# Latent attention on one core: product order and true widths of the narrow blocks

## The chip, the cores and the metric

The kernel runs on 1 core of a Trainium2 chip. The metric is the device time of one execution in microseconds (us), the median of several runs. Five engines work side by side and wait for each other by semaphores: PE multiplies matrices, DVE and ACT work on elements, POOL does a little of the same, SP issues the DMA transfers.

## The reference

Two layers of a decoder. Each normalises its input, projects it, sends it through three branches (a state-space mixer, latent attention, a gated DeltaNet), merges them by gates and ends with a feed-forward block. The change lies in the latent attention, which has 8 heads over 512 tokens in blocks of 128:

```python
sc = (jnp.einsum('bqhd,bkhd->bhqk', qn, k_nope, preferred_element_type=jnp.float32)
      + jnp.einsum('bqhr,bkr->bhqk', qp, k_pe, preferred_element_type=jnp.float32))
...
sc = jnp.where(kpos[None, :] <= qpos[:, None], sc * scale, -jnp.inf)
pr = jax.nn.softmax(sc, axis=-1)
return jnp.einsum('bhqk,bkhd->bqhd', pr.astype(v.dtype), v)
```

Two of the 192 score channels' parts matter below: 128 plain channels, and 64 rotated ones (`k_pe`, shared by all heads).

## The kernel before

All weights and activations are float32. A large product is made from three products of type float32r (float32 rounded to fewer mantissa bits): each operand is split into a high part (rounded by ACT) and a low part (the rest, by DVE), and high by high, high by low and low by high are added in PSUM. Lines 198 to 200 are these three products of the dense layers (`mm3`), lines 170 and 171 the two halves of a weight's split, lines 267 and 268 those of an activation's (`split_act`). Transposes and the small products of the other branches are in plain float32.

The latent attention of a layer works on four pairs of heads (`hp` 0 to 3). For a pair, three dense products give the plain queries of both heads and their rotary part (`pp`). The rotary part goes through a chain of its own: ACT scales it (`qp`, line 620), four DMAs swap its halves (line 545, inside `rope`), DVE rotates it (547 to 549), two DMAs move its 64 rows to the other half of the partitions (line 625), and ACT and DVE put the stacked operands `qps` and `qpl` together (629 to 631). Then keys and values are computed, and each head of the pair goes through these steps:

- Scores: for query block t = 0 to 3, five float32r products (lines 662 to 666) add into one PSUM bank over the first (t + 1) x 128 keys. Lines 665 and 666 are the rotary ones and read `qps` and `qpl`. For t = 0 the products cover 256 keys, of which the second 128 are not used afterwards.
- Softmax: DVE adds the causal mask and takes the extremum (671), ACT the exponential with its sum (673), DVE the reciprocal and the scaling (674, 675). The tile of block t is `pn` t.
- Transposes (683): ten blocks of 128 x 128 in three groups by key block: key block 0 (four of them), key block 1 (three), and key blocks 3 and 2 together (three).
- Split of each group into `th` and `tl` (267, 268): the tiles `mix` for key blocks 0 and 1, the tiles `pt` for blocks 3 and 2.
- Values: for each key block three float32r products (699 to 701) add into the bank `yt`, over the query blocks from that key block on: 512, 384 and 256 columns. Key block 3 has 128 true columns. `pt` has 128 zeroed columns ahead of them (line 577), and the products of block 3 cover 256.

In all there are 4 pairs, 2 heads and 2 layers, so 16 passes of these steps. The order of the instructions on each engine isn't the order of the code. A scheduler sets it when the kernel is built, from its own estimates of each instruction and from priorities: products that are ready at that time, above all the dense products of the next pair or the next branch, are put between the products of a head that still has to wait. SP issues its DMAs in one row, and one that waits for its buffer holds up those behind it. Weights are loaded into `wraw`, which has two buffers.

Line 570 is used as a measuring mark in the prediction: it is four plain float32 products of one column each per layer:

```python
for t in range(T):
    behind(((ly, "q", 0), 3, 2), pe.matmul(ps[:, t : t + 1], cq_sq[0][:, t * P : (t + 1) * P], ones[:, 0:1], start=True, stop=True))
```

Of the kernel before, what the change touches and what calls it, by code (L numbers as in the profile page):

```python
# [11 lines left out]
F32R = mybir.dt.float32r  # L12
# [8 lines left out]
P = 128  # L21
S = 512
T = S // P
# [32 lines left out]
def hybrid_kernel(ctx, tc, a, out, depth=2, taps=None):  # L56
    nc = tc.nc
    pe, act, dve, pool, sync = nc.tensor, nc.scalar, nc.vector, nc.gpsimd, nc.sync
    uid = itertools.count()

    def mk(pl, shape, dt, tag, bufs=None):
        return pl.tile(shape, dt, tag=tag, name=f"{tag}_{next(uid)}", bufs=bufs)
# [5 lines left out]
    def f32(ap):  # L68
        return ap.bitcast(F32)
# [195 lines left out]
    def split_act(hi, lo, src):  # L265
        with tc.high_priority(30):
            act.copy(hi, src)
            dve.tensor_tensor(lo, src, f32(hi), ALU.subtract)
# [112 lines left out]
    for ly in range(depth):  # L381
# [172 lines left out]
        ps = sm_bank()  # L554
# [17 lines left out]
        rsq(q_rs, ps[:, :T], 1.0 / 512, EPS)  # L572
        dve.tensor_scalar(q_rs, q_rs, -1.0, None, ALU.mult)

        pts = [mk(ml, [P, S], F32R, f"pt{i}") for i in range(2)]
        for x in pts:
            pool.memset(f32(x[:, :P]), 0.0)

        qpl = [mk(ml, [P, S], F32R, f"qpl{j}") for j in range(2)]
        for j in range(2):  # L580
# [4 lines left out]
        for hp in range(4):  # L585
            def q_weights():
                for k0 in (0, 2):
                    raw = mk(wp, [P, 768], F32, "wraw", 2)
                    sync.dma_start(raw.rearrange("p (k n) -> p k n", k=2),
                                   a["mla_w_uq"][ly][k0 * P : (k0 + 2) * P, hp * 384 : (hp + 1) * 384].rearrange("(k p) n -> p k n", p=P))  # L590
                    for k in range(2):
                        rv = raw[:, k * 384 : (k + 1) * 384].rearrange("p (h n) -> p h n", h=2)
                        hi = mk(wp, [P, 384], F32R, "whi")
                        lo = mk(wp, [P, 384], F32R, "wlo")
                        nv = lambda x: x[:, :256].rearrange("p (h n) -> p h n", h=2)
                        pv = lambda x: x[:, 256:].rearrange("p (h n) -> p h n", h=2)
                        act.copy(nv(hi), rv[:, :, :P])
                        act.copy(pv(hi), rv[:, :, P:])
                        dve.tensor_tensor(nv(lo), rv[:, :, :P], f32(nv(hi)), ALU.subtract)
                        dve.tensor_tensor(pv(lo), rv[:, :, P:], f32(pv(hi)), ALU.subtract)  # L600
                        yield k0 + k, hi.unsqueeze(1), lo.unsqueeze(1)

            *pq, pp = dense_F(q_weights(), tiles(384), 512, cqh, cql, tag=(ly, "q", hp))

            def head_tiles(pss, nm, c=None):
                res = []
                for ps in pss:
                    hi = mk(ml, [P, S], F32R, nm + "h", 3)
                    lo = mk(ml, [P, S], F32R, nm + "l", 3)
                    if c is None:  # L610
                        split_act(hi, lo, ps)
                    else:
                        act.mul(hi, ps, c)
                        dve.scalar_tensor_tensor(lo, ps, c, f32(hi), ALU.mult, ALU.subtract)
                    res.append((hi, lo))
                return res

            qs = head_tiles(pq, "q", scale)
            qp = mk(ml, [P, S], F32, "qp")
            act.mul(qp, pp, scale)  # L620
            qr = rope(qp)

            qd = mk(lp, [P, S], F32, "mix", 8)
            for i in range(2):
                sync.dma_start(qd[64 * i : 64 * i + 64], qr[64 * (1 - i) : 64 * (1 - i) + 64])
            qps = [mk(ml, [P, S], F32R, f"qps{j}") for j in range(2)]
            for j in range(2):
                half, other = (slice(64 * i, 64 * i + 64) for i in (j, 1 - j))
                act.copy(qps[j][half], qr[half])
                dve.tensor_tensor(qpl[j][half], qr[half], f32(qps[j][half]), ALU.subtract)  # L630
                act.copy(qps[j][other], qd[other])
            wkv = list(weights(a["mla_w_ukv"][ly], hp * 512, 512, 256))
            with tc.high_priority(30):
                ks = head_tiles(dense_F(wkv, [slice(0, P), slice(256, 256 + P)], 256, ckh, ckl), "k")

            vs = []
            for j in range(2):
                if hp % 2 == 0:
                    v2 = [mk(ml, [P, S], F32R, nm, 2) for nm in ("vh", "vl")]
                elif hp == 1:  # L640
                    v2 = [mk(lp, [P, S], F32R, f"y{e}{6 + j}") for e in "hl"]
                else:
                    v2 = [mk(ml, [P, S], F32R, f"cq{e}{j}") for e in "hl"]
                vs.append([x.rearrange("p (t n) -> p t n", t=T) for x in v2])

            def ev(t, ps):
                for j in range(2):
                    split_act(*(x[:, t, :] for x in vs[j]), ps[:, j * P : (j + 1) * P])

            vcols = lambda w: w.rearrange("p (h n) -> p h n", h=2)[:, :, P:]  # L650
            dense_T(wkv, 256, 256, ckh, ckl, ev, vcols)

            for j in range(2):
                qh, ql = qs[j]
                kh, kl = ks[j]
                pn = []
                for t in range(T):
                    n = max(256, (t + 1) * P)
                    tok = slice(t * P, (t + 1) * P)
                    ps = sm_bank()  # L660
                    o = ps[:, :n]
                    pe.matmul(o, qh[:, tok], kh[:, :n], start=True, stop=False)
                    pe.matmul(o, qh[:, tok], kl[:, :n], start=False, stop=False)
                    pe.matmul(o, ql[:, tok], kh[:, :n], start=False, stop=False)
                    pe.matmul(o, qps[j][:, tok], kps[:, :n], start=False, stop=False)
                    pe.matmul(o, qpl[j][:, tok], kph[:, :n], start=False, stop=True)
                    n = (t + 1) * P
                    o = ps[:, :n]
                    mx = mk(sp, [P, 1], F32, "mx", 8)
                    pt_ = mk(ml, [P, (t + 1) * P], F32, f"pn{t}", 2)  # L670
                    dve.tensor_tensor_reduce(pt_[:, :n], o, causal[:, S - n :], q_rs[:, t : t + 1], 3.0e38, ALU.add, ALU.min, mx)
                    sm = mk(sp, [P, 1], F32, "sme", 8)
                    act.activation(pt_[:, :n], pt_[:, :n], AF.Exp, bias=mx, scale=-1.0, accum_out=sm)
                    dve.reciprocal(sm, sm)
                    dve.tensor_scalar(pt_[:, :n], pt_[:, :n], sm, None, ALU.mult)
                    pn.append(pt_)
                po = y_bank()
                for kbs in ((0,), (1,), (3, 2)):
                    ps = sm_bank()
                    n = 0  # L680
                    for kb in kbs:
                        for t in range(kb, T):
                            pe.transpose(ps[:, n : n + P], pn[t][:, kb * P : (kb + 1) * P], ident)
                            n += P
                    if len(kbs) == 1:
                        th = mk(lp, [P, n], F32R, "mix", 8)
                        tl = mk(lp, [P, n], F32R, "mix", 8)
                        split_act(th, tl, ps[:, :n])
                        parts = [(kbs[0], kbs[0] * P, 0)]
                    else:  # L690

                        th, tl = pts
                        split_act(th[:, P:], tl[:, P:], ps[:, :n])
                        parts = [(2, 2 * P, 2 * P), (3, 2 * P, 0)]
                    for kb, c0, c in parts:
                        v_h, v_l = (x[:, kb, :] for x in vs[j])
                        o = po[:, c0:]
                        w = S - c0
                        pe.matmul(o, v_h, th[:, c : c + w], start=kb == 0, stop=False)
                        pe.matmul(o, v_h, tl[:, c : c + w], start=False, stop=False)  # L700
                        pe.matmul(o, v_l, th[:, c : c + w], start=False, stop=kb == T - 1)
                yh[2 * hp + j], yl[2 * hp + j] = (mk(lp, [P, S], F32R, f"y{e}{2 * hp + j}") for e in "hl")
                split_act(yh[2 * hp + j], yl[2 * hp + j], po)
                tap(f"oT{2 * hp + j}", f32(yh[2 * hp + j]))
            if hp == 0:
                dec, ndec, beta, dtq, dsk = step_sizes()
# [762 lines left out]
```

## Time and profile before

| | us |
|---|---|
| median of 3 runs (2276.94 to 2280.28) | 2278.16 |
| time of the profiled execution | 2278.48 |
| its span, first to last instruction | 2276.7 |
| latent attention, first layer (about 60 to 200 of the span) | 140 |
| latent attention, second layer (about 1190 to 1325) | 135 |

In the rows of a timeline the first number is the start in us from the span's start, the second the duration; `x5` means five instructions shown as one row. The brackets at a row's end say how long the engine was idle ahead of it and what ended the wait. Products overlap in PE's pipeline, so the pace of a stream of them is read from one start to the next and not from the durations. Line numbers are those of the kernel before.

### The profile page before, as it was taken

What the parts mean: (1) busy time and instruction counts of PE and PEld (TensorE: products, weight loads), DVE (VectorE), ACT (ScalarE), POOL (GpSimd) and SP (SyncE); (2) the same over time, 40 slices, a digit from 0 to 9 for tenths busy, and PEclk for the clock granted to TensorE, in tenths of its full rate; (3) what the DMA queues carried; (4) which work ended last, traced back from release to release, by engine and by line L of the source; (5) the groups of instructions that cost most, each with busy time, mean ns of one, the idle gap of its engine ahead of it and who ended that gap; (6) DMA issues with size and microseconds to landing.
All of it is one profiled execution on the core that took longest, in us unless ns stands there. A gap on an engine that the chain in (4) does not pass through costs nothing. (4 is left out here: it accounts for less than half of the span.)

```text
span 2276.7 us, 32125 instructions
## 1 busy us (share of the span) xinstructions
PE 2254.7 (99%) x11758; PEld 1868.6 (82%) x11758; DVE 1647.8 (72%) x3315; ACT 1182.9 (52%) x2444; POOL 65.0 (3%) x84
## 2 busy tenths in 40 slices
PE   9999999999999999999999999999999999999998
PEld 8888787888888888888888878888888887888886
DVE  7786567876667778767868865678657667778668
ACT  6666744333443465554656667443335445645545
POOL 1000000000000000000010000000001000000000
PEclk9999999999999999999999999999999999999999
DMA  4223634452225143233132236335422251432231
GB/s 143 81 75 102 195 102 121 129 148 75 83 68 176 56 148 111 91 99 117 48 104 81 70 113 202 96 118 148 121 84 75 66 184 38 167 111 101 85 111 47
DMA packets 220030, 244.07 MB, mean 107 GB/s; under 512 B 34256, under 2 KB 172384, under 8 KB 219872
## 3 DMA queue, kind: packets, MB, share of 16 engines
q1 hardware_dynamic: 219872, 242.02, 34.6%
q8 instruction: 92, 1.51, 0.3%
q14 instruction: 66, 0.54, 0.1%
HBM read 225.53 MB, written 11.74 MB: 104 GB/s over the span
## 5 line engine op out<-in xcount | busy, mean ns | idle before, releaser
L170 ACT CAST whi<-wraw 128x512 fp32r<-128x512 f32 (+1 forms) x536 | 329.3, 618 | 536.6 <-PE acc L199 357.4
L171 DVE TENSOR_TENSOR wlo<-wraw,whi 128x512 fp32r<-128x512 f32 (+1 forms) x536 | 364.9, 686 | 334.9 <-ACT whi L170 328.3
L198 PE MATMUL acc<-xh,whi 128*128 128x512 f32 (+1 forms) x1344 | 525.5, 392 | 0.0
L200 PE MATMUL acc<-xh,wlo 128*128 128x512 f32 (+1 forms) x1344 | 520.1, 387 | 0.8 <-DVE wlo L171 0.8
L199 PE MATMUL acc<-xl,whi 128*128 128x512 f32 (+1 forms) x1344 | 519.3, 387 | 0.0
L200 PEld LDWEIGHTS acc<-xh,wlo 128*128 128x128 f32 x1344 | 252.5, 188 | 50.5 <-DVE wlo L171 1.2
L199 PEld LDWEIGHTS acc<-xl,whi 128*128 128x128 f32 x1344 | 252.9, 188 | 47.9 <-DVE xl L272 0.7
L198 PEld LDWEIGHTS acc<-xh,whi 128*128 128x128 f32 x1344 | 252.4, 188 | 48.0 <-ACT xh L271 0.4
L170 ACT CAST whi<-wr 128x512 fp32r<-128x512 f32 x168 | 104.3, 621 | 107.9 <-PE acc L199 47.7
L198 PE MATMUL acc<-yh,whi 128*128 128x512 f32 x384 | 152.1, 400 | 0.0
L199 PE MATMUL acc<-yl,whi 128*128 128x512 f32 x384 | 150.3, 391 | 0.0
L200 PE MATMUL acc<-yh,wlo 128*128 128x512 f32 x384 | 149.8, 390 | 0.0
L171 DVE TENSOR_TENSOR wlo<-wr,whi 128x512 fp32r<-128x512 f32 x168 | 113.2, 686 | 35.5 <-ACT whi L170 34.7
L724 DVE SCALAR_TENSOR_TENSOR ckl<-acc,pc,ckl 128x511 f32<-128x511 f32 (+2 forms) x168 | 121.4, 743 | 19.6 <-ACT ckl L720 10.7
L198 PEld LDWEIGHTS acc<-yh,whi 128*128 128x128 f32 x384 | 71.5, 188 | 16.4 <-ACT yh L271 2.3
L200 PEld LDWEIGHTS acc<-yh,wlo 128*128 128x128 f32 x384 | 72.1, 188 | 15.1
L199 PEld LDWEIGHTS acc<-yl,whi 128*128 128x128 f32 x384 | 72.2, 188 | 14.3
L198 PE MATMUL acc<-whi,xh 128*128 128x512 f32 (+1 forms) x208 | 79.7, 385 | 0.0
L199 PE MATMUL acc<-wlo,xh 128*128 128x512 f32 (+1 forms) x208 | 79.3, 381 | 0.0
L200 PE MATMUL acc<-whi,xl 128*128 128x512 f32 (+1 forms) x208 | 78.8, 382 | 0.0
L484 ACT ACTIVATE eE<-eE,cum 128x128 f32<-128x128 f32 x192 | 62.8, 390 | 28.6 <-DMA eE<-d_c 28.6
L1209 DVE TENSOR_TENSOR h<-h,acc 128x512 f32<-128x512 f32 x120 | 77.0, 680 | 0.0
(461 smaller groups left out, 4499.4 us busy)
## 6 DMA issues: line engine op xcount, KB each, us to landing
wraw<-in_w_in_dram SPq DMA_DIRECT2D x144, 512.0 KB, 3.6
wraw<-in_w_up_dram SPq DMA_DIRECT2D x64, 512.0 KB, 3.5
wr<-in_w_down_dram SPq DMA_DIRECT2D x32, 1024.0 KB, 5.0
eE<-d_c SPq DMA_DIRECT2D x48, 256.0 KB, 4.3
wraw<-in_w_mla_out_dram SPq DMA_DIRECT2D x16, 512.0 KB, 3.3
eE<-d_e SPq DMA_DIRECT2D x32, 256.0 KB, 3.1
wraw<-in_w_ssd_out_dram SPq DMA_DIRECT2D x16, 512.0 KB, 3.4
wraw<-in_w_gdn_out_dram SPq DMA_DIRECT2D x16, 512.0 KB, 3.3
```

Of the source, the lines that this page charges most:

```text
L170: act.copy(hi, raw)
L171: dve.tensor_tensor(lo, raw, f32(hi), ALU.subtract)
L198: pe.matmul(o, ah, bh, start=start, stop=False, skip_group_check=more)
L199: pe.matmul(o, ah, bl, start=False, stop=False, skip_group_check=more)
L200: return pe.matmul(o, al, bh, start=False, stop=stop, skip_group_check=more)
L484: act.activation(o[:, i], o[:, i], AF.Relu, scale=-1.0, bias=cum[:, t, h0 + i : h0 + i + 1])
L724: dve.scalar_tensor_tensor(acc[:, d:], ps[:, : S - d], taps_[3 - d], acc[:, d:], ALU.mult, ALU.add)
L1209: dve.tensor_tensor(hs_, hs_, ps[t], op)
```

## The change

The score products of query block 0 cover 128 keys instead of 256. The value products of key block 3 cover 128 columns instead of 256; `pt` loses its zeroed columns, and the two fills of line 577 go. The three value products of a key block come in the order high by high, low values by high probabilities, high values by low probabilities; before, the last two stood the other way round.

```diff
-        pts = [mk(ml, [P, S], F32R, f"pt{i}") for i in range(2)]
-        for x in pts:
-            pool.memset(f32(x[:, :P]), 0.0)
+        pts = [mk(ml, [P, S - P], F32R, f"pt{i}") for i in range(2)]
...
-                    n = max(256, (t + 1) * P)
+                    n = (t + 1) * P
...
-                    n = (t + 1) * P
-                    o = ps[:, :n]
...
-                        split_act(th[:, P:], tl[:, P:], ps[:, :n])
-                        parts = [(2, 2 * P, 2 * P), (3, 2 * P, 0)]
+                        split_act(th, tl, ps[:, :n])
+                        parts = [(2, 2 * P, P), (3, 3 * P, 0)]
...
                         pe.matmul(o, v_h, th[:, c : c + w], start=kb == 0, stop=False)
-                        pe.matmul(o, v_h, tl[:, c : c + w], start=False, stop=False)
-                        pe.matmul(o, v_l, th[:, c : c + w], start=False, stop=kb == T - 1)
+                        pe.matmul(o, v_l, th[:, c : c + w], start=False, stop=False)
+                        pe.matmul(o, v_h, tl[:, c : c + w], start=False, stop=kb == T - 1)
```

The scheduler makes another order of the whole program of it, the same in both layers. Three places matter. In the changed kernel's rows, lines 660 to 664 are lines 662 to 666 of before, 679 is 683, 623 is 625, 587 is 589, and 695 to 697 are 699 to 701.

PE, second head of the third pair, from the last five transposes to the value products. `acc` rows are dense products of the next pair's keys and values. Before:

```order
L683 MATMUL sm_1808<-ct_75,pn_431_1765 128x128
L683 MATMUL sm_1808<-ct_75,pn_435_1778 128x128
L699 MATMUL yt_1784<-mix_1790,vh_1594 128x512
L700 MATMUL yt_1784<-mix_1791,vh_1594 128x512
L701 MATMUL yt_1784<-mix_1790,vl_1595 128x512
L699 MATMUL yt_1784<-mix_1801,vh_1594 128x384
```

And in the changed kernel:

```order
L679 MATMUL sm_1806<-ct_75,pn_431_1763 128x128
L679 MATMUL sm_1806<-ct_75,pn_435_1776 128x128
L200 MATMUL acc_1930<-ckh_138_657,wlo_1926 128x512
L198 MATMUL acc_1955<-whi_1921,ckh_137_656 128x256
L199 MATMUL acc_1955<-wlo_1922,ckh_137_656 128x256
L200 MATMUL acc_1955<-whi_1921,ckl_139_658 128x256
L695 MATMUL yt_1782<-mix_1788,vh_1592 128x512
L696 MATMUL yt_1782<-mix_1788,vl_1593 128x512
L198 MATMUL acc_1956<-whi_1921,ckh_137_656 128x256
L199 MATMUL acc_1956<-wlo_1922,ckh_137_656 128x256
L200 MATMUL acc_1956<-whi_1921,ckl_139_658 128x256
L697 MATMUL yt_1782<-mix_1789,vh_1592 128x512
```

Four dense products now stand between the last transpose and the first value product. The product with the low probabilities (`mix_1789`) comes after the one with the low values and four more dense products, of which three are shown.

SP, from the third pair's weights to the fourth pair's rotary DMAs: `wraw` rows are weight loads, 545 and 625 the rotary DMAs. Before:

```order
L589 DMA wraw_1859<-in_mla_w_uq_dram 128x2x384
L177 DMA wraw_1921<-in_mla_w_ukv_dram 128x2x512
L545 DMA mix_1540<-qp_1538 32x512 x4
L177 DMA wraw_2197<-in_w_in_dram 128x8x128
L625 DMA mix_1549<-mix_1545 64x512 x2
L177 DMA wraw_2239<-in_w_in_dram 128x8x128
L177 DMA wraw_2288<-in_w_in_dram 128x4x256
L177 DMA wraw_2322<-in_w_in_dram 128x4x256
L545 DMA mix_1901<-qp_1899 32x512 x4
L625 DMA mix_1910<-mix_1906 64x512 x2
```

And in the changed kernel:

```order
L587 DMA wraw_1857<-in_mla_w_uq_dram 128x2x384
L545 DMA mix_1538<-qp_1536 32x512 x4
L177 DMA wraw_1919<-in_mla_w_ukv_dram 128x2x512
L623 DMA mix_1547<-mix_1543 64x512 x2
L177 DMA wraw_2195<-in_w_in_dram 128x8x128
L177 DMA wraw_2237<-in_w_in_dram 128x8x128
L177 DMA wraw_2286<-in_w_in_dram 128x4x256
L545 DMA mix_1899<-qp_1897 32x512 x4
L177 DMA wraw_2320<-in_w_in_dram 128x4x256
L623 DMA mix_1908<-mix_1904 64x512 x2
```

The swaps (545) of the third and fourth pair now stand one weight load further forward.

PE, first head of the first pair, from the last score products to the first transpose. Before:

```order
L665 MATMUL sm_907<-kps_572,qps_170_780 128x512
L666 MATMUL sm_907<-kph_571,qpl_147_687 128x512
L198 MATMUL acc_1209<-ckh_137_656,whi_1201 128x512
L198 MATMUL acc_1102<-cqh_92_455,whi_1154 128x512
L683 MATMUL sm_921<-ct_75,pn_193_875 128x128
```

And in the changed kernel:

```order
L663 MATMUL sm_905<-kps_572,qps_170_778 128x512
L664 MATMUL sm_905<-kph_571,qpl_147_685 128x512
L200 MATMUL acc_1102<-cqh_91_454,wlo_1138 128x512
L679 MATMUL sm_919<-ct_75,pn_193_873 128x128
```

One dense product instead of two now covers the end of the softmax of block 0.

## The prediction

> **What bounds the kernel now.** I read the page first, then PE's busy time by stage, then the timeline of the attention.
>
> ```profile
> span 2276.7 us, 32125 instructions
> PE 2254.7 (99%) x11758; PEld 1868.6 (82%) x11758; DVE 1647.8 (72%) x3315; ACT 1182.9 (52%) x2444; POOL 65.0 (3%) x84
> PEclk9999999999999999999999999999999999999999
> ```
>
> PE is busy 99% of the span at its full granted clock. So only what shortens PE's stream of products, or a stop in it, moves the end; what DVE, ACT and POOL save counts only where PE waits for it. The stages, from the view of stretches (the second number is PE's busy time):
>
> ```profile
> 60.00:200.00 140.00, 138.51 (x765) 117.20 (x765) 111.27 (x296) 92.44 (x239) 1.01 (x1) 1.00 0.30 87
> 1190.00:1325.00 135.00, 133.13 (x737) 112.68 (x736) 107.06 (x290) 88.31 (x229) 1.01 (x1) 1.00 0.30 86
> 200.00:600.00 400.00, 399.07 (x2332) 326.11 (x2331) 268.42 (x542) 185.21 (x371) 10.32 (x10) 1.00 0.42 123
> ```
>
> The two attention stages show 1.5 and 1.9 us idle. That understates it, because a product counts as busy until it leaves the pipeline; what a stop costs is read from the starts. The stage behind the first attention, where the new order also moves products, has 0.9 us idle in 400, so there is little to win there.
>
> The pace of full streams, from the first products of each score block (timeline of PE; t = 0 and 1, then t = 2, t = 3, and what follows):
>
> ```profile
> 87.06 0.28 PE L662 MATMUL sm<-kh,qh 128*128 128x256 f32 x1
> ...
> 87.66 0.28 PE L662 MATMUL sm<-kh,qh 128*128 128x256 f32 x1
> ...
> 88.26 0.34 PE L662 MATMUL sm<-kh,qh 128*128 128x384 f32 x1
> ...
> 89.13 0.39 PE L662 MATMUL sm<-kh,qh 128*128 128x512 f32 x1
> ...
> 90.28 0.40 PE L199 MATMUL acc<-cql,whi 128*128 128x512 f32 x1
> ```
>
> Five products each: 0.12 us a product at 256 columns, 0.174 at 384, 0.23 at 512. Each 128 columns cost 0.055.
>
> **The narrow products.** Five score products and three value products in 16 passes, 128 in all, go from 256 columns to 128. No float32r product of 128 columns is in the trace. The line through the three paces gives 0.065, a gain of 0.055 x 128 = 7.0 us. But each product loads its own 128 x 128 operand first, and the load has a pace of its own. The mark is line 570, four products of one column, which leave nothing but loads:
>
> ```profile
> 65.85 1.09 PEld L570 LDWEIGHTS sm<-ct,pn 128*128 128x128 f32 x8
> 66.08 0.95 PE L570 MATMUL sm<-ct,pn 128*128 128x1 f32 x8
> ...
> 66.89 0.47 PE L200 MATMUL acc<-ckh,wlo 128*128 128x512 f32 x1
> ```
>
> Eight loads and eight products stand for the four of the code: a plain float32 product is two. They take 66.89 - 66.08 = 0.81 us, 0.10 each; by the loads, (1.09 - 0.19) / 7 = 0.13. So a load of this size holds the pace at about 0.11. Loads for float32r have the same length as plain ones of the same size, and the length grows with the columns loaded:
>
> ```profile
> L662 PEld LDWEIGHTS sm<-kh,qh 128*128 128x128 f32 x64 | 12.1, 190 | 1.4 <-DVE mx L671 1.1
> L987 PEld LDWEIGHTS sm<-tok,tok 64*64 64x64 f32 x128 | 8.0, 135 | 2.8 <-issue 2.8
> ```
>
> 190 - 135 = 55 ns for 64 columns, so 0.11 us for 128. I take 0.11 for a narrow product: it has the same load, and the load is the larger of its two parts. That is 0.01 x 128 = 1.3 us saved. The upper end is the pace of plain float32 products of 128 columns, two passes each:
>
> ```profile
> 580.49 0.60 PE L1050 MATMUL sm<-ft,ft 128*128 128x128 f32 x4
> 580.93 1.06 PE L1067 MATMUL sm<-tok,tok 128*128 128x128 f32 x8
> 581.74 0.48 PE L198 MATMUL acc<-xh,whi 128*128 128x512 f32 x1
> ```
>
> Twelve passes in 1.25 us are 0.104 each, about 0.21 a product and with the mark's 0.11 up to 0.22: a loss of 0.10 x 128 = 12.8 us. Both ends stay for the range.
>
> The Trainium skill's page "TensorE: Matmul & The Clock Gate", section "Back-to-back issue gap", gives about 81 ns for a product of 128 columns in a stream with loads. By that the saving would be an estimated 0.039 x 128 = 5.0 us instead of 1.3. The same sentence has 131 ns for 512 columns, and here those take 230, so I give it little weight.
>
> **The value products' order.** Where a head has no other work to put between, PE stops twice: for ACT's `th`, and one product later for DVE's `tl`. In the second head of the third pair, in each layer:
>
> ```profile
> 151.17 0.71 PE L683 MATMUL sm<-ct,pn 128*128 128x128 f32 x5
> 152.58 0.50 PE L699 MATMUL yt<-mix,vh 128*128 128x512 f32 x1 [0.70 <-ACT mix L267]
> 153.42 0.50 PE L700 MATMUL yt<-mix,vh 128*128 128x512 f32 x1 [0.34 <-DVE mix L268]
> 153.76 0.40 PE L701 MATMUL yt<-mix,vl 128*128 128x512 f32 x1
> ...
> 1279.63 0.71 PE L683 MATMUL sm<-ct,pn 128*128 128x128 f32 x5
> 1281.05 0.49 PE L699 MATMUL yt<-mix,vh 128*128 128x512 f32 x1 [0.70 <-ACT mix L267]
> 1281.89 0.50 PE L700 MATMUL yt<-mix,vh 128*128 128x512 f32 x1 [0.35 <-DVE mix L268]
> ```
>
> Five transposes are 0.55 at 0.11 each, so line 699 starts 152.58 - 151.17 - 0.55 = 0.86 late; line 700 comes 0.84 behind it instead of 0.23, 0.61 late; line 701 0.11. That is 1.58, and the second layer has the same. In the new order (front part, first place) four products stand ahead of the first value product, 0.23 + 3 x 0.12 = 0.59, and cover that much of the 0.86. Between it and the product with `tl` stand the one with the low values and four more, 0.23 + 4 x 0.12 = 0.71 beyond the 0.23 that were there, more than the 0.61. What stays is 0.27 and the 0.11 that a stop adds: 0.38. Saved 1.2, in two layers 2.4 us. If the filling work is missing later, the ends are 0 and 3.2.
>
> **The rotary wait.** The rescheduling also moves the chain to `qps`. The group row of that wait at the loads, and the two products around the longest case:
>
> ```profile
>   ACT qps L631: 4.1, 7
> ...
> 1263.07 0.39 PE L198 MATMUL acc<-cqh,whi 128*128 128x512 f32 x1
> 1264.09 0.39 PE L665 MATMUL sm<-kps,qps 128*128 128x256 f32 x1 [0.63 <-ACT qps L631]
> ```
>
> Line 665 comes 1.02 behind its forerunner, 0.79 late. All seven waits are 4.1 us at the loads, which run ahead of the products; PE loses perhaps half, 2.0. What makes the chain late is SP's row, shown for the fourth pair, beside the first pair, where the chain runs free:
>
> ```profile
> 66.28 0.60 ACT L620 ACTIVATE qp<-acc 128x512 f32<-128x512 f32 x1 [0.38 <-PE acc L200]
> 66.90 3.39 SPq L545 DMA_DIRECT2D mix<-qp  x4
> 76.74 1.26 ACT L631 CAST qps<-mix 64x512 fp32r<-64x512 f32 x2
> ...
> 141.50 0.60 ACT L620 ACTIVATE qp<-acc 128x512 f32<-128x512 f32 x1
> 141.91 11.25 SPq L177 DMA_DIRECT2D wraw<-in_w_in_dram  x2
> 153.26 2.45 SPq L545 DMA_DIRECT2D mix<-qp  x4
> ```
>
> Free, it takes 76.74 + 0.63 - 66.28 = 11.1 us to the first head's `qps`. For the fourth pair the swap was issued 153.26 - 142.10 = 11.2 late, behind a weight load that waited for its buffer. In the new order the swaps stand ahead of that load (second place), and by the paces above 12.4 to 13.8 us of products stand between the end of the rotary query product and line 665. That covers 11.1, so I take the 2.0 as saved; the ends are 4.1 and a loss of 2, should one of the three later chains of a layer be held up by 1 us.
>
> **What it adds.** With one product less ahead of the first transpose (third place), 2.17 us of products lie between line 665's first and that transpose instead of 2.41; in the trace DVE had `pn` 0 ready 2.32 behind it:
>
> ```profile
> 78.23 0.28 PE L665 MATMUL sm<-kps,qps 128*128 128x256 f32 x1
> 80.27 0.28 DVE L675 TENSOR_SCALAR pn<-pn,sme 128x128 f32<-128x128 f32 x1
> ```
>
> 80.27 + 0.28 - 78.23 = 2.32, so 0.15 of new wait in up to four heads of a layer, eight in all, 1.0 us with the cases that escape it. The four fills of `pt` on POOL (line 577) go; POOL is busy 3%, and PE waits for none of them: nothing. ACT and DVE split the same widths as before, and every product that is not narrowed stays.
>
> **The sum.** -1.3 - 2.4 - 2.0 + 1.0 = -4.7 us. From the profiled execution, 2278.5 (1.8 of it outside the span), that gives 2273.8; the median of the runs is 0.3 lower, 2278.2, so I say 2273.5, which is 0.2% faster. About 0.2%, 4.6 us, is also what a measurement of this kernel can tell from no change, so the forecast lies on that edge.
>
> **Rivals.**
> 1. Narrow float32r products run at the plain rate, slower than before. Its place is the first score block and the fourth key block of all 16 passes; the price 0.22 instead of 0.12 us, +12.8. With the waits' -3.4 that is +9.4, 2287.6. It decides from 0.12 + 3.4 / 128 = 0.147 us a product on, and shows as slower by over 0.2% from 0.18 on. For it speaks that no float32r product below 256 columns is in the trace, so nothing shows that the fast rate holds there; against it that the three widths lie on one line with no sign of a step.
> 2. Loads don't hold the narrow products back, and they run on the line at 0.065: -7.0 - 3.4 = -10.4, 2267.8. Against it stand the one-column products at 0.10. The skill's 81 ns, named above, lies between the two.
> 3. The waits are only moved: what the rescheduling saves at the value products and `qps` it loses at softmax and transposes, and only the 1.3 of the narrow products stay: 2276.9. For it speaks that in most other heads the stop for `th` is short and has the same one to three fillers as before.
>
> **Chances.** The forecast 0.60, its own range 2271 to 2276 (half of the two waits' saving missing, or the new wait absent and the loads a little quicker); rival 1 0.20, rival 2 0.08, rival 3 0.12. The range must hold four fifths, so it has to reach into rival 1: 2269 to 2288 leaves out rival 2 and the upper part of rival 1, together under 0.2. Faster by over 0.2% (below 2273.6): half of the forecast, 0.32, and rival 2, 0.40. Slower (above 2282.7): 0.20, rival 1. The rest, 0.40, is within.
>
> **What would show it.** Starts of lines 662 to 666 at t = 0 and of the key block 3 products 0.11 us apart: the load bound; 0.065: rival 2; 0.2 or more: rival 1. Value products of the second head of the third pair with no stop for DVE's `mix`, and one under 0.4 us for ACT's: the second term. No wait of over 0.3 us at `qps`, and the fourth pair's swap issued within 2 us of `qp`: the third. New waits for `pn` at the first transpose: the fourth. The prediction is wrong if the narrow pace is above 0.15, or if a rotary chain is still late although its swap stands earlier.

## The result and the profile after

The changed kernel takes 2284.57 us (median of 9 runs, 2283.42 to 2286.06), the kernel before 2279.37 (9 runs): a ratio of 1.0021, 95% interval 1.0012 to 1.0029. It is 5 us slower; the prediction was 2273.5, 0.2% faster. Its range, 2269 to 2288, does hold the time, but only through the part that was added for slow narrow products. The profiled execution took 2283.78. Times of one kernel differ from chip to chip by some tenths of a us, so below the ratios to the kernel before are compared, each from runs on one chip.

The head of the page and the attention stages (second number PE's busy time):

```profile
span 2282.0 us, 32137 instructions
PE 2254.4 (99%) x11758; PEld 1863.9 (82%) x11758; DVE 1650.2 (72%) x3315; ACT 1183.4 (52%) x2444; POOL 64.5 (3%) x80
...
60.00:200.00 140.00, 136.75 (x753) 113.38 (x752) 110.53 (x294) 92.90 (x241) 1.01 (x1) 1.00 0.30 86
1190.00:1325.00 135.00, 130.66 (x726) 108.80 (x725) 105.05 (x286) 87.59 (x229) 1.01 (x1) 1.00 0.29 82
```

PE's busy time is the same within 0.3 us, and the span is 5.3 longer. PE is idle for 3.25 of 140 us instead of 1.49 in the first attention, and for 4.34 of 135 instead of 1.87 in the second. So the loss is idle time of PE. The narrow widths do take a little off PE's busy time when the order is held (2256.3 with wide products in the changed order, from a run below, against 2254.4 here), but new stops cost more. The groups of PE say which; the last part of a row is the idle time ahead and what ended it. Before:

```profile
L198 PE MATMUL acc<-xh,whi 128*128 128x512 f32 x1280 | 507.8, 397 | 0.0
L683 PE MATMUL sm<-ct,pn 128*128 128x128 f32 x160 | 28.0, 276 | 0.0
L665 PE MATMUL sm<-kps,qps 128*128 128x256 f32 x32 | 9.2, 298 | 1.1 <-ACT qps L631 0.9
L699 PE MATMUL yt<-mix,vh 128*128 128x512 f32 x8 | 4.0, 500 | 1.5 <-ACT mix L267 1.4
L700 PE MATMUL yt<-mix,vh 128*128 128x512 f32 x8 | 3.4, 422 | 0.7 <-DVE mix L268 0.7
```

And the changed kernel (663 is 665 of before, 679 is 683, 695 and 697 are 699 and 700):

```profile
L198 PE MATMUL acc<-xh,whi 128*128 128x512 f32 x1280 | 508.0, 397 | 2.2 <-DVE cql L268 2.2
L679 PE MATMUL sm<-ct,pn 128*128 128x128 f32 x160 | 28.9, 280 | 2.0 <-DVE pn L671 1.9
L663 PE MATMUL sm<-kps,qps 128*128 128x128 f32 x16 | 4.8, 300 | 2.7 <-ACT qps L629 2.6
L695 PE MATMUL yt<-mix,vh 128*128 128x512 f32 x8 | 3.9, 493 | 0.0
L697 PE MATMUL yt<-mix,vh 128*128 128x512 f32 x8 | 3.2, 394 | 0.0
```

The stops of the value products went, 2.2 us. In their place stand 2.2 at a dense product, 2.0 at the transposes, and 1.6 more at `qps`. These idle times understate a stop, because a product still in the pipeline counts as busy. So I also added up stops from the starts: over both attention stages (60 to 200 and 1188 to 1330), how much later each product starts than the pace of the one ahead allows (0.11 us for a transpose and for 128 columns, 0.12, 0.17 and 0.23 for 256, 384 and 512; gaps under 0.015 left out, and most lags of about 0.1 that a dense product has behind a transpose or a stop). That sum is 12.5 us before and 18.5 after. With all those lags counted it is 18.5 before and 25.1 after, a difference of 6.6 instead of 6.0: what is counted shifts all sums together, and a difference by about 1. By kind, before and after: transposes waiting for `pn` 1.1 and 5.2, products waiting for `qps` 1.8 and 3.7, the first dense products of the next branch 0.4 and 2.6, the value products 5.4 and 3.2.

### The profile page after: what moved, and what is told of

Same layout as the page of the kernel before. It is cut to its first block, busy times and chain, and to the rows that moved or that the text cites. A ratio compares the mean times of both kernels' runs of the same rounds, so it can differ in the third digit from the quotient of the medians.

```text
span 2282.0 us, 32137 instructions
## 1 busy us (share of the span) xinstructions
PE 2254.4 (99%) x11758; PEld 1863.9 (82%) x11758; DVE 1650.2 (72%) x3315; ACT 1183.4 (52%) x2444; POOL 64.5 (3%) x80
## 5 line engine op out<-in xcount | busy, mean ns | idle before, releaser
L199 PEld LDWEIGHTS acc<-yl,whi 128*128 128x128 f32 x384 | 72.2, 188 | 14.2
```

The costliest lines, as they stand in the source:

```text
L199: pe.matmul(o, ah, bl, start=False, stop=False, skip_group_check=more)
```

## The experiments

Theory O says that the loss comes from the order that the scheduler made of the changed code; rival P, that it lies in the new products themselves: in their widths (W in the first four expectations) or in the order of the value products (V). The letters of the later expectations stand for other theories and are explained there.

**Parts of the change in the old order, and the new order with the old products.** Here PE, DVE, ACT and SP are held in a given order: ahead of scheduling, each engine's instructions are tied in a row by dependencies that only order them. `PIN` is a table with the order of the kernel before or of the changed one.

```diff
+    pinned(tc, PIN)
...
+        for a, b in zip(row, row[1:]):
+            tc.add_manual_dep(b, a.name, how, reason="pinned")
```

Narrow widths alone, old order:

> Both narrowings (score block 0 and key block 3 over 128 columns) with the value products in the old order, and every instruction of PE, DVE, ACT and SP held in the place it has in the kernel before, so that only the widths differ. Theory O (the loss of the change comes from the new order that the scheduler made, not from the products): 0 to 2 us faster than before, a narrow product at 0.10 to 0.12 us. Rival W (the narrow products themselves cost more than the wide ones, for instance by slowing the product behind them): slower by 2 to 5 us.

New value order alone, old order:

> Only the order of the second and third value product is changed, all widths as before, every other instruction in the place it has in the kernel before. Theory O: 0.5 us faster at most (the wait for the low probabilities in the second head of the third pair shrinks from 0.61 us by the 0.23 of the product that now stands ahead of it, in two layers; elsewhere nothing waits), so 0 to 0.6 us. Rival V (the order of the value products costs by itself, for instance because the same loaded operand no longer comes twice running): slower by 2 us or more.

Both, old order:

> The whole change, but every instruction of PE, DVE, ACT and SP in the place it has in the kernel before (second and third value product exchanged in their places). Theory O: 0 to 2.5 us faster than before, so 5 to 8 us faster than the changed kernel. Rivals W or V: as slow as the changed kernel, 4 to 6 us over before.

Widths of before, new value order, the changed kernel's order:

> The other way round: the wide products of before (256 columns) and their zeroed columns, but the value products' order and the place of every instruction on PE, DVE, ACT and SP as in the changed kernel. Theory O: as slow as the changed kernel or a little slower, 4 to 7 us over before. Rivals W or V: W says at most 2 us over before, V 4 to 6.

Measured: 0.9993 (0.9984 to 1.0002), 0.9997 (0.9988 to 1.0006), 0.9991 (0.9983 to 1.0000), and 1.0020 (1.0011 to 1.0029). The new order with the old widths is as slow as the changed kernel; the whole change in the old order isn't slower than before. That is theory O; rival P falls, in both its forms: each part alone in the old order is no slower than before. No run holds the changed kernel in its own order and alters nothing else; since the wide one held in that order is as slow as the free kernel (1.0020 and 1.0021), holding as such costs nothing that shows here. Which engine's row carries the loss was not tried. The groups of both parts in the old order, and of the wide one in the new (held kernels have other line numbers: 688 and 690 are the score products with `qps`, 704 and 708 the transposes, 223 the dense product):

```profile
L223 PE MATMUL acc<-xh,whi 128*128 128x512 f32 x1280 | 507.8, 397 | 0.0
L704 PE MATMUL sm<-ct,pn 128*128 128x128 f32 x160 | 27.9, 276 | 0.0
L688 PE MATMUL sm<-kps,qps 128*128 128x128 f32 x16 | 4.5, 281 | 0.9 <-ACT qps L654 0.7
```

```profile
L223 PE MATMUL acc<-xh,whi 128*128 128x512 f32 x1280 | 507.9, 397 | 2.2 <-DVE cql L293 2.2
L708 PE MATMUL sm<-ct,pn 128*128 128x128 f32 x160 | 28.9, 280 | 1.8 <-DVE pn L700 1.7
L690 PE MATMUL sm<-kps,qps 128*128 128x256 f32 x32 | 9.5, 307 | 3.5 <-ACT qps L656 3.4
```

All three new stops come with the order, whatever the widths.

**Which part of the change makes that order?** Each part alone, the scheduler free (the diff of the change, cut to the widths or to the exchange of the two value products).

> Narrow widths only (score block 0 and key block 3 over 128 columns), the value products in the order of before, and the scheduler free to make its own order. Theory W (the narrow widths make the scheduler choose the late order, and the order costs the time): the order of its rows stands nearer to the changed kernel's, the swaps of the fourth pair stand ahead of the weight load as there, so 2283 us (2281 to 2285). Rival B (the late order needs both parts of the change together): as the narrow widths in the old order, 2277.7, at most 2279. Rival V (the exchanged value products are what moves the order): 2277.7 as well, and then the run with the value order alone is the late one.

> Value products in the new order only, all widths as before, the scheduler free. Theory W: its order stays near that of before, 2278.5 us (2277 to 2280). Rival V (the exchange moves the order): 2283 (2281 to 2285).

Measured: narrow widths 1.0014 (1.0005 to 1.0023), value order 0.9986 (0.9977 to 0.9995). Groups of the first, then of the second:

```profile
L198 PE MATMUL acc<-xh,whi 128*128 128x512 f32 x1280 | 507.6, 397 | 0.0
L679 PE MATMUL sm<-ct,pn 128*128 128x128 f32 x160 | 28.8, 279 | 2.0 <-DVE pn L671 1.9
L663 PE MATMUL sm<-kps,qps 128*128 128x128 f32 x16 | 4.7, 293 | 0.5 <-ACT qps L629 0.3
```

```profile
L683 PE MATMUL sm<-ct,pn 128*128 128x128 f32 x160 | 28.6, 279 | 0.0
L665 PE MATMUL sm<-kps,qps 128*128 128x256 f32 x32 | 9.1, 295 | 1.0 <-ACT qps L631 0.9
```

The widths alone bring the stops at the transposes, and the swaps of the third and fourth pair stand ahead of a weight load as in the changed kernel, which was theory W's sign. The stops at the dense product, and those added at `qps`, come only with both parts together, as rival B has it. The times don't say how the loss divides. The median of the widths alone, 2282.08, is in W's range, but its eleven times go from 2278.52 to 2284.51, and the profiled execution is the fastest of them: its span, 2276.7, is that of the kernel before, with the stops at the transposes in it. What makes the other executions longer is in no trace here and stays open. The value order alone, 2275.59, was missed by both expectations: it gets a third order, faster than the kernel before.

**What each stop is worth.** In the changed kernel's order, PE is made not to wait for the rotary chain, for softmax, or for both; shapes, number and order of products stay.

```diff
-                    pe.matmul(o, qps[j][:, tok], kps[:, :n], start=False, stop=False)
-                    pe.matmul(o, qpl[j][:, tok], kph[:, :n], start=False, stop=True)
+                    pe.matmul(o, kph[:, tok], kps[:, :n], start=False, stop=False)
+                    pe.matmul(o, kps[:, tok], kph[:, :n], start=False, stop=True)
...
-                            pe.transpose(ps[:, n : n + P], pn[t][:, kb * P : (kb + 1) * P], ident)
+                            pe.transpose(ps[:, n : n + P], incl, ident)
```

> The changed kernel, every instruction of PE, DVE, ACT and SP held in the changed kernel's order; the two rotary score products read the key operands in place of qps and qpl, so PE does not wait for the rotary chain (the rotary part of the scores is left out). Same number, shapes and order of products. Theory S (the loss is the sum of PE's stops, each worth its own length): the stops at qps and the product behind it, 3.7 + 0.85 us in the trace of the changed kernel, go: 2284.6 - 4.5 = 2280 us (2279 to 2281.5). Rival M (a stop that is taken away comes back at the next wait, since softmax or the next split is then the limit): 2283 to 2284.6, with longer waits at the first transpose or the value products in its trace.

> The changed kernel, every instruction held in the changed kernel's order; the transposes read a constant block in place of pn, so PE does not wait for the softmax (the probabilities are left out of the values). Same number, shapes and order of products. Theory S: the stops at the first transposes, 5.2 us in the trace of the changed kernel, go: 2284.6 - 5.2 = 2279.4 us (2278.5 to 2281). Rival M (the stop moves on to the value products, which still wait for ACT and DVE): 2283 to 2284.6, with the waits for the split at the value products up by the same amount.

> The changed kernel, every instruction held in its order, with both edits of the last two runs: rotary score products read the key operands, transposes read a constant block (rotary part and probabilities are left out). Theory S (the two waits add up, 4.5 and 5.3 us as measured one by one): 2284.6 - 9.8 = 2274.8 us, 2273.5 to 2276.5. Rival M (each of them removed alone already took the same later wait with it): 2278 to 2280.

Measured: 1.0005 (0.9996 to 1.0014), 1.0001 (0.9993 to 1.0010) and 0.9990 (0.9981 to 0.9999). Against the changed kernel's 1.0021, times 2279, that is 3.6 us for the rotary stops, 4.6 for those at softmax and 7.1 for both, each uncertain by about 3. The medians of the single runs, 2280.06 and 2279.33, are within theory S's ranges. That of both together, 2277.28, is in neither: S had 2273.5 to 2276.5, M 2278 to 2280. One by one the savings add to 8.2, which the 7.1 do not contradict within the error, but M is right in part: without the rotary wait, the stops at the transposes grow from 5.2 to 6.7.

**Does the missing cover make the stops at the transposes?** In the changed order, 0 or 1 dense products stand ahead of the first transpose of a head (in the kernel before 2 to 4 in the first head of a pair, 0 or 1 in the second), and none to 2 ahead of the second transpose. The edit moves those that stand right behind the first three transposes ahead of them (d a dense product, T a transpose; first head, second head):

```diff
- d T d T T d d d d d
+ d d d T T T d d d d
...
- T T T d d d d d
+ d d T T T d d d
```

> The changed kernel, its own order on DVE, ACT and SP, and on PE but for one thing in all 16 heads: the dense products that stand right behind the first three transposes are put ahead of them, so that three products in the first head of a pair and two in the second cover the softmax, in place of one and none. Nothing is left out or added, and what stands from the fourth transpose on starts no later. Theory C (the waits at the first transposes come from the missing cover): 5.2 us of waits for pn fall to about 1, as in the kernel before, so 2284.6 - 4 = 2280.6 us, 2279.5 to 2282. Rival D (softmax itself is late in this order, or the wait moves to the value products): 2283 to 2285.

Measured: 1.0013 (1.0005 to 1.0022), 1.8 us less than the changed kernel by the ratios, 3.1 by the medians (2281.45). The group and one head, behind the last score products:

```profile
L679 PE MATMUL sm<-ct,pn 128*128 128x128 f32 x160 | 26.6, 278 | 0.3
...
91.47 0.39 PE L199 MATMUL acc<-ckl,whi 128*128 128x512 f32 x1
91.70 0.60 PE L679 MATMUL sm<-ct,pn 128*128 128x128 f32 x3
...
92.60 0.40 PE L198 MATMUL acc<-ckh,whi 128*128 128x512 f32 x1
93.06 0.44 PE L679 MATMUL sm<-ct,pn 128*128 128x128 f32 x2
```

The stop at the first transposes is gone (91.70 is 0.23 behind the product ahead). At the next two (93.06) 0.23 has come instead: from 92.60, one product of 0.23 would end at 92.83. From the starts, all waits for `pn` are 3.3 instead of 5.2, not 1 as theory C had it. So more cover takes away the first stops, as theory C has it, and rival D is right in part: products put in front of one block are missing in front of the next. The median is within C's range, 2279.5 to 2282.

**The stop at the dense product.** In the fourth pair, the split that frees its bank stands on DVE behind the rotation, which waits for the swap's DMA. The edit puts that one split ahead in each layer:

```diff
- L171 wlo<-wraw,whi; L548 mix<-mix,sinT; L268 cql<-acc,cqh
+ L268 cql<-acc,cqh; L171 wlo<-wraw,whi; L548 mix<-mix,sinT
```

> The changed kernel, its own order on every engine, but for one split on DVE in each layer's fourth pair: the low part of the first 128 columns of the next product's bank (L268, tile cql) is put ahead of the weight split and of the rotation (L548) that it stood behind, so that the bank of the dense product comes free 1.1 us sooner. Theory Q (the rotary chain of that pair sets the pace of this place, and the dense products only fill the time ahead of it): the 2.2 us of waits of acc<-xh,whi for DVE go, but the wait at qps grows by nearly as much, from 2.6 to about 4.7 us in the group row, so the time stays: 2284.6 us (2283 to 2286). Rival A (the two stops add up, each is worth its length): 2284.6 - 2.2 = 2282.4 us (2281.5 to 2283), with the wait at qps as it was.

```profile
L198 PE MATMUL acc<-xh,whi 128*128 128x512 f32 x1280 | 508.4, 397 | 0.5 <-DVE cql L268 0.5
L663 PE MATMUL sm<-kps,qps 128*128 128x128 f32 x16 | 4.8, 300 | 3.6 <-ACT qps L629 3.5
```

Of 1.7 us saved at the dense product, 0.9 come back at `qps`, which is between Q and A. The time is 1.0016 (1.0007 to 1.0025), median 2281.89: as A expects by the median, 1.1 us under the changed kernel by the ratios. With intervals that overlap, this run doesn't decide; the rows show that about half of the stop moved on.

**A better kernel.** The whole change, held in the order that the scheduler made for the value order alone.

> The whole change (narrow widths and new value order), with PE, DVE, ACT and SP held in the order that the scheduler made for the value order alone. Theory O (the order decides; the narrow widths by themselves are worth what they were in the old order, 1.4 us): 2275.6 - 1.4 = 2274.2 us, 2273 to 2275.5, faster than both kernels. Rival N (narrow widths lose by themselves, since score blocks end sooner and softmax is then the limit): 2277 or more, with longer waits for pn in the trace.

Measured: 2274.46 us, 0.9980 (0.9971 to 0.9989), faster than both kernels and within theory O's range. From the value order alone (0.9986) it can't be told apart. Its groups have none of the three stops left above 0.6 us:

```profile
L198 PE MATMUL acc<-xh,whi 128*128 128x512 f32 x1280 | 508.1, 397 | 0.0
L679 PE MATMUL sm<-ct,pn 128*128 128x128 f32 x160 | 28.6, 279 | 0.0
L663 PE MATMUL sm<-kps,qps 128*128 128x128 f32 x16 | 4.4, 272 | 0.6 <-ACT qps L629 0.5
```

**All kernels together**: the sum of stops in the two attentions from the starts, and the time against the kernel before (ratio less 1, times 2279 us).

| kernel | stops, us | time, us |
|---|---|---|
| wide products, changed order | 19.2 | +4.6 |
| changed kernel | 18.5 | +4.8 |
| split first | 17.7 | +3.6 |
| narrow widths, free order | 16.1 | +3.2 |
| more cover | 16.1 | +3.0 |
| no rotary wait | 15.3 | +1.1 |
| no softmax wait | 14.6 | +0.2 |
| narrow widths, old order | 13.0 | -1.6 |
| value order, old order | 12.9 | -0.7 |
| before | 12.5 | 0 |
| both, old order | 12.0 | -2.1 |
| value order, free order | 10.8 | -3.2 |
| neither wait | 10.6 | -2.3 |
| both, order of the value order's run | 10.0 | -4.6 |

The best line through the 14 points has 0.98 us of time for 1 us of stops, and no point lies more than 1.3 off it, which is within the error of a ratio. With all lags counted, it has 0.99 and no point is more than 1.7 off. Two limits belong to this. The sums are from one execution of each kernel, the times from medians: against the spans of the same executions the line has 1.02, but more cover lies 3.4 above it and the narrow widths in a free order 2.7 below. And of that kernel's 16.1 us, 2.2 are waits for `tok` in the convolution of the state-space branch (line 753), which its order puts within the two stretches; without them its time lies 3.0 above the line, so the stops in the attention don't explain it. The four kernels with wide products lie on both sides of it: what the widths are worth by themselves is too small to see here.

## Why the prediction was wrong

**The narrow products (-1.3): right in pace and size.** Eight in a row, and the score block behind them:

```profile
86.28 0.22 PE L695 MATMUL yt<-pt,vh 128*128 128x128 f32 x1
86.34 0.28 PE L696 MATMUL yt<-pt,vl 128*128 128x128 f32 x1
...
86.56 0.28 PE L660 MATMUL sm<-kh,qh 128*128 128x128 f32 x1
...
87.12 0.33 PE L660 MATMUL sm<-kh,qh 128*128 128x256 f32 x1
87.30 0.28 PE L661 MATMUL sm<-kl,qh 128*128 128x256 f32 x1
...
87.77 0.34 PE L660 MATMUL sm<-kh,qh 128*128 128x384 f32 x1
```

The five score products take 0.56, 0.112 each, the three value products 0.28: 0.06 for the first and 0.11 for the others. That is near the 0.10 to 0.13 of the mark, as a pace set by the loads would be; no run tries the loads by themselves. Rivals 1 (0.2 or more) and 2 (0.065) fall, and so does the saving of 5.0 us that the prediction gives as an estimate. But the five products of 256 columns behind them take 0.65 instead of the 0.60 of before: the first of them takes 0.18, the other four 0.12 each. A pass saves 8 x 0.12 - 0.84 - 0.05 = 0.07 us, sixteen save 1.1. In the old order the widths measured 1.6 faster, within 2.

**The value products (-2.4): right.** The same place after:

```profile
150.27 0.48 PE L695 MATMUL yt<-mix,vh 128*128 128x512 f32 x1
150.59 0.40 PE L696 MATMUL yt<-mix,vl 128*128 128x512 f32 x1
...
151.30 0.40 PE L697 MATMUL yt<-mix,vh 128*128 128x512 f32 x1
```

No stop for ACT's `mix` ahead of the first (it comes 0.12 behind a product of 256 columns) and none for DVE's; only 0.09 is left behind the first (0.32 to the next start, less 0.23), where 0.38 was expected. That is 1.5 less in each layer, so elsewhere the value products lost 0.8: from the starts they stop PE for 3.2 instead of 5.4 in all, 2.2 less.

**The rotary wait (-2.0): the wrong sign, and the first step that failed: the length of the chain.** The swap stands earlier, as foreseen: issued 1.35 behind the start of `qp` in the fourth pair. The chain is late all the same, which the prediction named as what would make it wrong:

```profile
148.63 0.60 ACT L618 ACTIVATE qp<-acc 128x512 f32<-128x512 f32 x1
149.98 2.45 SPq L545 DMA_DIRECT2D mix<-qp  x4
156.25 0.68 DVE L548 TENSOR_TENSOR mix<-mix,sinT 128x512 f32<-128x512 f32 x1
161.50 1.26 ACT L629 CAST qps<-mix 64x512 fp32r<-64x512 f32 x2 [0.78 <-DMA mix<-mix]
162.82 0.33 PE L663 MATMUL sm<-kps,qps 128*128 128x128 f32 x1 [0.49 <-ACT qps L629]
```

In the kernel before, the same score product started 0.42 behind the product ahead, 0.2 late:

```profile
165.59 0.39 PE L199 MATMUL acc<-xl,whi 128*128 128x512 f32 x1
166.01 0.39 PE L665 MATMUL sm<-kps,qps 128*128 128x256 f32 x1
```

The prediction held a chain of 11.1 us against 12.4 to 13.8 us of products. The products were right: from the start of `qp` to the score product it is 14.2 us here, a wait of 0.65 included, so a room of 13.5. The chain's length was not. The 11.1 is the first pair's, where DVE and ACT are free, and goes up to the end of the first of two casts (629, before 631). PE starts 0.05 behind the end of the second one, here and in every pair of both layers; that alone adds 0.6. And in this pair the rotation (548) starts 6.3 behind the swap's issue, and from its end to the last casts go 4.6. So the chain takes 161.50 + 1.26 - 148.63 = 14.1, and in the second and third pairs 12.7 to 14.5.

The swap's earlier place did what it should: the fourth pair's chain took 24.5 before. But the new order took the room away with it. `qp` starts at 148.63 instead of 141.50, because the rotary query product stands later, and the score product comes at 162.82 instead of 166.01: a room of 13.5 instead of 24.3. PE waited for the second cast in five of the eight pairs before, now in all eight, and the longest stop, in the third pair of the second layer, was 1.8:

```profile
1265.55 0.33 PE L663 MATMUL sm<-kps,qps 128*128 128x128 f32 x1 [1.65 <-ACT qps L629]
```

The term came out as +1.9 from the starts instead of -2.0 (3.7 instead of 1.8).

**The new wait at the transposes (+1.0): the second step that failed: when `pn` is ready.** The head that the prediction looked at, the first:

```profile
77.36 0.33 PE L663 MATMUL sm<-kps,qps 128*128 128x128 f32 x1
79.81 0.53 DVE L671 TENSOR_SCALAR pn<-pn,sme 128x128 f32<-128x128 f32 x2
80.13 0.33 PE L679 MATMUL sm<-ct,pn 128*128 128x128 f32 x1 [0.24 <-DVE pn L671]
```

It took `pn` 0 as ready 2.32 behind the first score product with `qps`, as in the old order. Here it is ready at 79.81 + 0.28, 2.73 behind: the new order of DVE puts both scalings (671) behind the reciprocal of block 1. The products ahead of the transpose last 2.37 and not 2.17, so with `pn` at 2.32 the lost product of cover alone would have cost nothing; that a wait came where the term has one is partly luck. It is 0.40. And a head that it did not look at, the second of the first pair:

```profile
89.57 0.39 PE L664 MATMUL sm<-kph,qpl 128*128 128x512 f32 x1
89.80 0.27 PE L679 MATMUL sm<-ct,pn 128*128 128x128 f32 x1
90.44 0.44 PE L679 MATMUL sm<-ct,pn 128*128 128x128 f32 x2 [0.38 <-DVE pn L671]
```

The second transpose starts 0.64 behind the first instead of 0.11. The prediction took 0.15, for the first transpose alone. In the second heads of two pairs nothing at all stands between the scores and the first three transposes, and it is the second one that waits. The term measured 4.1 (5.2 instead of 1.1).

**What had no term.** The dense product that stops 1.3 us in each layer's fourth pair (+2.1 from the starts), since the split that frees its bank stands behind a rotation on DVE:

```profile
157.28 0.47 PE L198 MATMUL acc<-xh,whi 128*128 128x512 f32 x1 [1.12 <-DVE cql L268]
```

By measured sizes the sum is -1.1 - 2.2 + 1.9 + 4.1 + 2.1 = +4.8, as much as the ratio gives, whose own error is 2. Rival 3, that waits are only moved, was the right idea with the wrong end: it took their sum as unchanged, and it grew by 6. The chance of 0.20 for slower, and the range up to 2288, were given for a reason, slow narrow products, that wasn't the one: that the range holds the time is luck.

## What to carry to other kernels

When a scheduler reorders a program after an edit, the edit's own cost and the new order's are two questions: hold the order and measure the edit, then hold the edit and measure the order. Compare the new order at every repetition of a place and on every engine that feeds it, PE's own row for the producer too; one head and one queue showed a gain where sixteen heads held a loss. A small edit that an unlucky order makes slower can be kept with an order found elsewhere: here the same change is 0.2% slower in one order and 0.2% faster in another.

## What was not expected

The sum of PE's stops in two stages that are 12% of the span goes with the median time of 14 kernels within 1.3 us, although PE's busy share is 99% in all of them; for one of them, the narrow widths in a free order, only with waits of another branch counted in.

The paces of narrow and wider products are not simply added where they meet. In the changed kernel's trace the first narrow product behind one of 256 columns takes only 0.06 (18 places), and the first of 256 columns behind narrow ones 0.17 instead of 0.12 (26 places).

Behind the attention, in the convolution of the state-space branch, PE waits a varying time for DVE's `ft`; with more cover:

```profile
L745 PE MATMUL sm<-ct,ft 128*128 128x128 f32 x8 | 1.3, 280 | 3.0 <-DVE ft L280 3.0
```

With narrow widths and a free order it is 0.0, before 0.7, in the changed kernel 1.7, with both parts in the old order 0.9, without either wait 2.0. It follows none of the edits, and each number is from one execution. It may be part of why the times of one kernel spread by up to 6 us (more cover: 2279.6 to 2285.6): the trace with 3.0 is of an execution 3.2 us above its kernel's median, the one with 0.0 of one 3.6 below. Over the other twelve the two go together only weakly (a correlation of 0.43), and what sets the wait stays open.
